# Low halves of the weights made by a second pass of ScalarE and a DMA that adds, in one layer of a hybrid decoder on one core

## The chip, the core and the metric

The kernel runs on one core of a Trainium2 chip. A core has TensorE (PE, with a row of its own, PEld, for weight loads), VectorE (DVE), ScalarE (ACT), GpSimd (POOL), SyncE (SP) and 16 DMA engines that all queues share. Each engine works through its own queue in order. The metric is the time on the device in microseconds (us); less is better. Two runs of the kernel before took 1355.51 and 1356.83 us, median 1356.17.

## What is computed

One layer of a decoder for 512 tokens of 1024 features, everything in float32. Cut to its products:

```
h = h + 0.5 * swiglu(rms_norm(h, ffn1_norm[l]), ffn1_w_gu[l], ffn1_w_down[l])     # 1024 -> 2 x 2816 -> 1024
n = rms_norm(h, mix_norm[l])
p = n @ w_in[l] + b_in[l]                                                         # 1024 -> 6 x 1024
y_a = conformer_conv_branch(...)    # GLU, causal depthwise conv (31 taps), layer norm, swish, @ w_a_out
y_b = spatial_gating_branch(...)    # gelu, layer norm, 128x128 mixing over tokens, @ w_b_out
h = h + (sigmoid(g_a) * y_a + sigmoid(g_b) * y_b) @ w_out[l]
h = h + memory_cross_attention(...) # @ w_q; memory of 256 tokens @ w_kv; 4 heads; @ w_o
h = h + 0.5 * swiglu(rms_norm(h, ffn2_norm[l]), ffn2_w_gu[l], ffn2_w_down[l])
return rms_norm(h, final_norm)
```

## The kernel before

Activations lie transposed: features on the 128 partitions, the 512 tokens along the rows. TensorE works on a float32 form of reduced precision (`F32R`), so each operand is split into a high half (the value rounded to `F32R`) and a low half (the value minus its high half), and a product of two operands takes three matmuls (`mm3`, L103): high times high, high times low of the activations, low of the weights times high. The third of each K tile is the one that needs the weights' low half (L106; L173 in `linear_rows`).

The weights come in blocks of up to 128 x 1024 numbers (512 KB): eight K tiles of 128 columns, or two K tiles of 512 columns. `wload` (L100) does for each block what `wfetch` and `wsplit` do: a DMA on SP's queue into one of four `raw` buffers (L88), ScalarE's copy, rounded, into one of three `whi` buffers (L96), and VectorE's subtraction into one of three `wlo` buffers (L97). Each tile's name follows its product: `g3w0l` is the low half of the first block of the gate product 3. `part`, `linear` and `linear_rows` call `wload`; `linear_pair` and the first two pairs of products call `wsplit` themselves.

In order of time the products are: the gated up-projections g and u of the first half-step FFN (22 each; one block per product), its down-projections d (8; blocks of 1024, 1024 and 768 columns of `raw`), the memory's keys `pk0` to `pk5` (one block each, moving only 256 columns), the input projection (`av`, `ag` by features; `r` by tokens), the two last keys, the gates `gb`, the mixing over tokens, w_b (`yb`), the gates `ga`, the memory's values `pv` (eight blocks of two K tiles, for 256 tokens), w_a (`ya`), w_out (`o`), the queries `pq`, the heads with w_o between them (`wo`; some of its blocks are cut to 768, 512 or 256 columns so that they fit between the heads), and the second FFN. The convolution's 240 vector operations (L344) are spread over the blocks from `av` on by `spend` (L113), which counts a split of a block as 1.14 us of vector work.

A norm's `1/sqrt` is a `pow` of a few columns on GpSimd (L196), in the middle of a chain over PE, VectorE, GpSimd, VectorE, PE and ScalarE (`rstat`, L199). GpSimd's queue has otherwise nine DMAs in all: the mixing weights `wsr` and eight rows broadcast over the partitions (`br`, `gr`, `bb`; 256 KB each).

The order of each engine's queue is not that of the code line by line: a scheduler places the instructions by its own estimate of their lengths, so that it shifts where an operation changes.

Of the kernel before, what the change touches and what calls it, by code (L numbers as in the profile page):

```python
# [11 lines left out]
F32R = mybir.dt.float32r  # L12
AF = mybir.ActivationFunctionType
ALU = mybir.AluOpType
PSUM = bass.MemoryType.PSUM

P = 128
# [13 lines left out]
EPS_RMS = 1e-6  # L31
EPS_LN = 1e-5

# lengths that the order of issue goes by: a K tile's products of 512 columns, a block's split, a vector operation
MM_US, SPLIT_US, OP_US = 0.65, 1.14, 0.66

VECS = [("ffn1_norm", 8), ("mix_norm", 8), ("xattn_norm", 8), ("mem_norm", 8), ("ffn2_norm", 8),
# [10 lines left out]
def conformer_layer(ctx: ExitStack, tc: tile.TileContext, xT, memT, vecs, rows, w_gu1, w_dn1, w_in_f, w_in_t,  # L48
# [31 lines left out]
        return tmp.tile([P, n], dt, tag="ev", name=name, bufs=5)  # L80

    def wfetch(srcs, name):
        """the blocks [128, K tiles, 128 or 512 columns] one after the other in one tile"""
        raw = wpool.tile([P, 1024], F32, tag="raw", name=name, bufs=4)
        n = 0
        for src in srcs:
            m = src.shape[1] * src.shape[2]
            nc.sync.dma_start(out=raw[:, n:n + m], in_=src.rearrange("p k c -> p (k c)"))  # L88
            n += m
        return raw[:, :n]  # L90
# [7 lines left out]
        return hi.rearrange("p (k c) -> p k c", c=c), lo.rearrange("p (k c) -> p k c", c=c)  # L98

    def wload(src, name):  # L100
        return wsplit(wfetch([src], name), src.shape[2], name)

    def mm3(out, whi, wlo, ahi, alo, start, stop):  # L103
        PE.matmul(out, whi, ahi, start=start, stop=False)  # L104
        PE.matmul(out, whi, alo, start=False, stop=False)  # L105
        PE.matmul(out, wlo, ahi, start=False, stop=stop)  # L106

    # steps of vector work that may run at any time (generators that give each step's length) stand behind the
    # blocks of weights, as many as the products of a block leave room for; soon: in order, first; later: by turns
    soon, later = deque(), deque()  # L110
    room = [None]

    def spend(us):  # L113
        """vector work us long has been issued; positive room is filled with steps"""
        if room[0] is not None:
            room[0] = min(room[0], 4.0) - us
            while (soon or later) and room[0] > 0:
                steps = soon or later
                used = next(steps[0], None)
                if used is None:  # L120
                    steps.popleft()
                    continue
                room[0] -= used
                if steps is later and len(steps) > 1:
                    steps[0], steps[1] = steps[1], steps[0]
# [7 lines left out]
        return ps.tile([P, T], F32, tag="mm", name=name)  # L133

    def part(acc, wsrc, ahi, alo, k0, k1, name):
        """K tiles k0 to k1 of a product with wsrc [128, K tiles, 128 columns] stationary, activations moving."""
        nk = wsrc.shape[1]
        whi, wlo = wload(wsrc[:, k0:k1, :], f"{name}w{k0}")
        for k in range(k0, k1):
            mm3(acc, whi[:, k - k0, :], wlo[:, k - k0, :], ahi[k], alo[k], k == 0, k == nk - 1)  # L140
        spend(SPLIT_US - MM_US * (k1 - k0) * acc.shape[1] / T)

    def linear(wsrc, ahi, alo, name, n=T):
        """a whole product: PSUM tile [128 columns, n]"""
        nk = wsrc.shape[1]
        acc = new_ps(name)[:, :n]
        for k0 in range(0, nk, 8):
            part(acc, wsrc, ahi, alo, k0, min(nk, k0 + 8), name)
        return acc

    def linear_pair(wsrcs, ahi, alo, name):
        """two products side by side, K tile by K tile, for activations that come one by one"""
        accs = [new_ps(f"{name}{i}") for i in range(2)]
        for k0 in range(0, DT, DT // 2):
            ks = slice(k0, k0 + DT // 2)
            whi, wlo = wsplit(wfetch([w[:, ks, :] for w in wsrcs], f"{name}w{k0}"), P, f"{name}w{k0}")
            for k in range(k0, k0 + DT // 2):
                for i in range(2):
                    c = i * DT // 2 + k - k0
                    mm3(accs[i], whi[:, c, :], wlo[:, c, :], ahi[k], alo[k], k == 0, k == DT - 1)  # L160
        return accs

    def linear_rows(wsrc, ahi, alo, ntok, name):
        """activations stationary, wsrc [128, K tiles, 512 columns] moving: PSUM tiles [128 tokens, 512]."""
        nk = wsrc.shape[1]
        accs = [new_ps(f"{name}{t}") for t in range(ntok)]
        for k0 in range(0, nk, 2):
            whi, wlo = wload(wsrc[:, k0:k0 + 2, :], f"{name}w{k0}")
            for k in (k0, k0 + 1):
                for t in range(ntok):  # L170
                    a_h, a_l = ahi[k][:, t * P:(t + 1) * P], alo[k][:, t * P:(t + 1) * P]
                    PE.matmul(accs[t], a_h, whi[:, k - k0, :], start=k == 0, stop=False)  # L172
                    PE.matmul(accs[t], a_h, wlo[:, k - k0, :], start=False, stop=False)  # L173
                    PE.matmul(accs[t], a_l, whi[:, k - k0, :], start=False, stop=k == nk - 1)  # L174
            spend(SPLIT_US - MM_US * 2 * ntok)
        return accs
# [20 lines left out]
        return r  # L197

    def rstat(accs, n, eps, name, copy=True):  # L199
        """accs [128, n]: per partition sums of squares. 1/sqrt(mean + eps) as columns [128 tokens, n/128] and as  # L200
        rows on all partitions [128, n]."""
        nt = n // P
        pc = ps2.tile([P, T], F32, tag="st", name=name + "c")[:, :nt]
        for t in range(nt):
            for i, acc in enumerate(accs):
                PE.matmul(pc[:, t:t + 1], acc[:, t * P:(t + 1) * P], avg[:, 0:1], start=i == 0, stop=i == len(accs) - 1)
        ms = tmp.tile([P, TT], F32, tag="ms", name=name + "m", bufs=2)[:, :nt]
        V.tensor_scalar(out=ms, in0=pc, scalar1=eps, scalar2=None, op0=ALU.add)
        rc = pow_mhalf(ms, nt, name + "r")
        dg = ev(name + "d", n)  # L210
        for t in range(nt):
            V.tensor_scalar(out=dg[:, t * P:(t + 1) * P], in0=ident, scalar1=rc[:, t:t + 1], scalar2=None, op0=ALU.mult)
        pb = ps2.tile([P, T], F32, tag="st", name=name + "b")[:, :n]
        PE.matmul(pb, ones, dg, start=True, stop=True)
        if not copy:
            return rc, pb
        rb = tmp.tile([P, n], F32, tag=f"rb{n}", name=name + "rb", bufs=1)
        S.copy(out=rb, in_=pb)  # L218
        return rc, rb
# [2 lines left out]
        split_scaled(xhi[:, m, :], xlo[:, m, :], h[:, m, :], col(g, m))  # L222

    def prep(m, g, acc):
        """residual tile m is final: operands of the next product and its part of the norm."""
        split_x(m, g)
        add_square(acc, h[:, m, :], m == 0)

# [20 lines left out]
        return hi, lo  # L249

    def ffn_up(w_gu, rb, first=()):
        """the hidden activations, split; first: products of the first pairs that are already there"""
        f = [gate_up(pg, pu, rb, j) for j, (pg, pu) in enumerate(first)]
        for j in range(len(first), FT):
            pg = linear(w_gu[j], xh, xl, f"g{j}")
            pu = linear(w_gu[FT + j], xh, xl, f"u{j}")
            f.append(gate_up(pg, pu, rb, j))
        return [a for a, _ in f], [b for _, b in f]
# [1 line left out]
    def add_half(m, pd, ts=slice(0, T)):  # L260
        V.scalar_tensor_tensor(out=h[:, m, ts], in0=pd, scalar=0.5, in1=h[:, m, ts], op0=ALU.mult, op1=ALU.add)  # L261

    # the first two pairs of products go along with the loads, K tile by K tile
    HF = DT // 2
    raws = []
    for k in range(DT):
# [66 lines left out]
    aps, cv, done = [], {}, []  # L333

    def conv(i):
        """causal depthwise convolution of a channel tile; tap k reaches CW - 1 - k tokens back"""
        c = slot(f"cv{i}")
        cv[i] = c
        for back in range(CW):
# [8 lines left out]
            V.tensor_tensor(out=csum, in0=done[0] if len(done) == 2 else csum, in1=c, op=ALU.add)  # L348
        yield OP_US

    # gated channels
    room[0] = 0
    for i in range(DT):
        pv = linear(w_in_f[i], xh, xl, f"av{i}")
# [6 lines left out]
        spend(OP_US)  # L361
        later.append(conv(i))

    # spatial gating unit, tokens on partitions
    wsr = slot("wsr")
    nc.gpsimd.dma_start(out=wsr, in_=sgu_wT.rearrange("s g t -> s (g t)"))
    # [s, t]: kept where t >= s
    wsr3 = wsr.rearrange("s (g t) -> s g t", g=GROUPS)
    G.affine_select(out=wsr3, in_=wsr3, compare_op=ALU.is_ge, fill=0.0, base=0, pattern=[[0, GROUPS], [1, P]],
                    channel_multiplier=-1)  # L370
# [6 lines left out]
        return t  # L377

    def token_major(which):
        """gelu of 1024 columns of the input projection: tiles [token tile][column half]"""  # L380
        out = [[None, None] for _ in range(TT)]
        for half in range(2):
            br = row(which, half, f"br{which}{half}")
# [64 lines left out]
        obl.append(lo)  # L448
        spend(OP_US)

    # the rest of the keys and the values of the memory, and the steps of the spatial gating in between
    vts = [[None, None], [None, None]]

    def value(half):
# [26 lines left out]
            gate_b(TT + k // 2)  # L481
        transposed_u(k)

    # sigmoid(gate_B) * y_B
    for m in range(DT):
        py = linear(w_b[m], obh, obl, f"yb{m}")
        V.tensor_tensor(out=sgb[m], in0=py, in1=sgb[m], op=ALU.mult)
# [8 lines left out]
    finish(later)  # L496
    room[0] = None

    # layer norm over channels, swish
    pmean = ps2.tile([P, T], F32, tag="st", name="pmean")  # L500
    PE.matmul(pmean, avg, csum, start=True, stop=True)
    mean = ev("mean")
# [20 lines left out]
        aah.append(hi)  # L523
        aal.append(lo)

    # sigmoid(gate_A) * y_A, merge
    mgh, mgl = [], []
    py01 = linear_pair([w_a[0], w_a[1]], aah, aal, "ya")
    for m in range(DT):
# [40 lines left out]
        return hi, lo  # L570

    def softmax(hd):
        """probabilities [128 tokens, memory], two token tiles side by side"""
        out = []
        for t2 in range(0, TT, 2):
            sc = ps2.tile([P, 2, NM], F32, tag="st", name="sc")
# [49 lines left out]
            V.tensor_tensor(out=h[:, m, :], in0=po[m], in1=h[:, m, :], op=ALU.add)  # L626
            prep(m, "ffn2_norm", acc)

    # independent products stand between the steps of a head
    q = {}  # L630

    def fill(i):
# [26 lines left out]
    for m in range(last):  # L659
        add_half(m, linear(w_dn2[m], fh, fl, f"d{m}"))  # L660
        add_square(acc, h[:, m, :], m == 0)
        S.activation(h[:, m, :], h[:, m, :], AF.Copy, scale=col("final_norm", m))
    # the last product and the final norm by halves of the tokens
    ws = [wload(w_dn2[last][:, k0:min(FT, k0 + 8), :], f"dl{k0}") for k0 in range(0, FT, 8)]
    for i in range(2):
        ts = slice(i * T // 2, (i + 1) * T // 2)
# [74 lines left out]
```

## Time and profile before

| | |
|---|---|
| time, median of two runs | 1356.17 us |
| span of the profiled execution | 1355.1 us |
| PE busy | 1332.3 us (98%), 5968 matmuls |
| weight loads of PE busy | 1079.1 us (80%) |
| VectorE busy | 777.9 us (57%) |
| ScalarE busy | 456.5 us (34%) |
| GpSimd busy | 19.4 us (1%) |
| mean granted clock of TensorE | 0.996 |
| moved by DMA | 132.47 MB, mean 98 GB/s |

The span goes from the first to the last instruction of the profiled execution. "Busy" counts an engine's own operations; an engine that is 98% busy on the chain that ended last is what sets the time, as long as nothing else makes it wait. A row with `<-` names what a wait ended with.

### The profile page before, as it was taken

To read this page: it belongs to the slowest core of one execution; us is meant where nothing else is said; L and a number is where in the kernel's file an instruction comes from. 1 tells how busy PE (TensorE), PEld (TensorE's weight loads), DVE (VectorE), ACT (ScalarE), POOL (GpSimd) and SP (SyncE) were. 2 spreads that over 40 slices of the span, in tenths; PEclk is the share of its full clock that TensorE was granted. 3 is DMA by queue.
4 is the path that set the end of the run, shared out by engine and by line. 5 is a ranking of instruction groups with operands and counts; after the bars stand their busy time and mean duration, and the time that the engine had idled before them with its cause. 6 is when DMAs were issued, how large, how long until landed. Compare 5 with 4: busy or idle time off the path is not lost.

```text
span 1355.1 us, 14923 instructions
## 1 busy us (share of the span) xinstructions
PE 1332.3 (98%) x5968; PEld 1079.1 (80%) x5968; DVE 777.9 (57%) x1078; ACT 456.5 (34%) x618; POOL 19.4 (1%) x31
## 2 busy tenths in 40 slices
PE   7999999999999999999999999999999999999996
PEld 6788888888898888888787788887878888888886
DVE  5544444434367999998996775554644444442323
ACT  5322222223233223343224743334432222222221
POOL 0000000000020000100000000000000000000000
PEclk9999999999999999999999999999999999999998
DMA  6333333233353332322233333202332333323321
GB/s 207 109 94 93 94 93 94 86 96 109 114 181 115 94 94 94 101 97 76 92 94 116 102 109 109 62 20 76 123 93 93 94 94 93 94 86 101 86 70 62
DMA packets 40660, 132.47 MB, mean 98 GB/s; under 512 B 4432, under 2 KB 7248, under 8 KB 40592
## 3 DMA queue, kind: packets, MB, share of 16 engines
q1 hardware_dynamic: 39872, 129.17, 30.9%
q0 software_dynamic: 720, 2.36, 0.6%
q8 instruction: 46, 0.75, 0.2%
q14 instruction: 22, 0.18, 0.0%
HBM read 129.42 MB, written 2.10 MB: 97 GB/s over the span
## 4 chain that ended last, share of the span: by engine, by line
PE 97%; DVE 1%; ACT 1%; DMA 0%; issue 0%; SPq 0%; DVEq 0%; POOLq 0%; ACTq 0%
PE u L106 6%; PE g L104 6%; PE u L105 6%; PE g L105 6%; PE g L106 6%; PE u L104 6%; PE d L106 6%; PE d L104 6%; PE d L105 6%; PE r L173 2%; PE r L172 2%; PE r L174 2%; PE ya L104 1%; PE ya L105 1%; PE o L105 1%; PE av L105 1%
## 5 line engine op out<-in xcount | busy, mean ns | idle before, releaser
L344 DVE SCALAR_TENSOR_TENSOR cv<-ap,vec,cv 128x494 f32<-128x494 f32 (+24 forms) x240 | 163.3, 729 | 0.4
L244 DVE TENSOR_TENSOR u<-u,n4rb 128x512 f32<-128x512 f32 x22 | 15.2, 692 | 70.3 <-PE u L106 70.3
L244 DVE TENSOR_TENSOR u<-u,n1rb 128x512 f32<-128x512 f32 x20 | 13.8, 691 | 65.8 <-PE u L106 65.8
L240 DVE TENSOR_TENSOR g<-g,n4rb 128x512 f32<-128x512 f32 x22 | 15.2, 692 | 51.7 <-PE g L106 47.5
L240 DVE TENSOR_TENSOR g<-g,n1rb 128x512 f32<-128x512 f32 x20 | 13.8, 691 | 43.3 <-PE g L106 43.3
L246 DVE TENSOR_TENSOR f<-s,u 128x512 f32<-128x512 f32 x44 | 30.4, 692 | 5.4 <-ACT s L242 1.1
L261 DVE SCALAR_TENSOR_TENSOR h<-d,h 128x512 f32<-128x512 f32 x15 | 10.4, 692 | 31.5 <-PE d L106 31.5
L242 ACT ACTIVATE s<-g 128x512 f32<-128x512 f32 x44 | 27.8, 633 | 0.1
L192 DVE TENSOR_TENSOR acc<-acc,sq 128x512 f32<-128x512 f32 x34 | 23.3, 685 | 0.1
L191 ACT ACTIVATE sq<-h 128x512 f32<-128x512 f32 x34 | 21.2, 624 | 1.4 <-DVE h L261 0.2
L184 DVE SCALAR_TENSOR_TENSOR xlo<-h,vec,xhi 128x512 fp32r<-128x512 f32 x24 | 17.7, 746 | 5.3 <-ACT xhi L183 5.2
L183 ACT ACTIVATE xhi<-h,vec 128x512 fp32r<-128x512 f32 x24 | 17.2, 717 | 1.9 <-DVE h L626 1.0
L543 DVE TENSOR_TENSOR h<-o,h 128x512 f32<-128x512 f32 x8 | 5.5, 692 | 13.7 <-PE o L106 13.7
L532 DVE TENSOR_TENSOR ga<-ya,sga 128x512 f32<-128x512 f32 x8 | 5.5, 690 | 13.4 <-PE ya L106 13.4
L387 DVE TENSOR_TENSOR uv<-r,br 128x512 f32<-128x512 f32 x16 | 10.7, 686 | 0.1
L104 PE MATMUL fg<-xhi,first0h 128*128 128x512 f32 x4 | 2.2, 553 | 7.8 <-ACT first0h L96 7.8
L587 ACT ACTIVATE pr<-sc,mx 128x256 f32<-128x256 f32 x16 | 7.4, 470 | 6.4 <-DVE mx L584 6.3
L567 DVE TENSOR_TENSOR qt<-pq,n3rb 128x512 f32<-128x512 f32 x8 | 5.3, 687 | 7.3 <-ACT n3rb L218 4.3
L626 DVE TENSOR_TENSOR h<-wo,h 128x512 f32<-128x512 f32 x8 | 5.4, 688 | 7.0 <-PE wo L106 7.0
L388 ACT ACTIVATE uv<-uv 128x512 f32<-128x512 f32 x16 | 9.0, 621 | 0.6 <-DVE uv L387 0.6
L583 DVE TENSOR_REDUCE mx<-sc 128x2 f32<-128x512 f32 x8 | 5.5, 692 | 3.7 <-PE sc L106 3.3
L97 DVE TENSOR_TENSOR d1w8l<-d1w,d1w8h 128x1024 fp32r<-128x1024 f32 x2 | 2.5, 1226 | 8.7 <-ACT d1w8h L96 8.7
(4300 smaller groups left out, 4279.4 us busy)
## 6 DMA issues: line engine op xcount, KB each, us to landing
h<-xT SPq DMA_DIRECT2D x8, 256.0 KB, 5.9
first<-w_gu SPq DMA_DIRECT2D x8, 256.0 KB, 6.1
d0w<-w_dn SPq DMA_DIRECT2D x4, 512.0 KB, 3.5
d1w<-w_dn SPq DMA_DIRECT2D x4, 512.0 KB, 3.7
d2w<-w_dn SPq DMA_DIRECT2D x4, 512.0 KB, 3.4
d3w<-w_dn SPq DMA_DIRECT2D x4, 512.0 KB, 3.5
d4w<-w_dn SPq DMA_DIRECT2D x4, 512.0 KB, 3.6
d5w<-w_dn SPq DMA_DIRECT2D x4, 512.0 KB, 3.4
```

Source lines behind the costliest of these rows:

```text
L104: PE.matmul(out, whi, ahi, start=start, stop=False)
L105: PE.matmul(out, whi, alo, start=False, stop=False)
L106: PE.matmul(out, wlo, ahi, start=False, stop=stop)
L172: PE.matmul(accs[t], a_h, whi[:, k - k0, :], start=k == 0, stop=False)
L173: PE.matmul(accs[t], a_h, wlo[:, k - k0, :], start=False, stop=False)
L174: PE.matmul(accs[t], a_l, whi[:, k - k0, :], start=False, stop=k == nk - 1)
L192: V.tensor_tensor(out=acc, in0=acc, in1=sq, op=ALU.add)
L240: V.tensor_tensor(out=g1, in0=pg, in1=rb, op=ALU.mult)
L242: S.activation(s1, g1, AF.Silu)
L244: V.tensor_tensor(out=u1, in0=pu, in1=rb, op=ALU.mult)
L246: V.tensor_tensor(out=f, in0=s1, in1=u1, op=ALU.mult)
L344: V.scalar_tensor_tensor(out=o, in0=aps[i][:, :T - back], scalar=w, in1=o, op0=ALU.mult, op1=ALU.add)
```

## The change

`wload` no longer calls `wsplit`. ScalarE makes the high half as before, and then, in a second pass over the same block, the negative high half into the `wlo` buffer. A DMA issued from GpSimd's queue then reads the block of weights from memory once more and adds it to what lies in that buffer, which leaves the weights minus their high half. `linear_pair` and the first products keep `wsplit` with VectorE. Lines from `wload` on are seven further down.

```diff
     def wload(src, name):
-        return wsplit(wfetch([src], name), src.shape[2], name)
+        raw = wfetch([src], name)
+        n, c = raw.shape[1], src.shape[2]
+        hi = wpool.tile([P, 1024], F32R, tag="whi", name=name + "h", bufs=3)[:, :n]
+        lo = wpool.tile([P, 1024], F32R, tag="wlo", name=name + "l", bufs=3)[:, :n]
+        S.copy(out=hi, in_=raw)
+        S.activation(lo, raw, AF.Copy, scale=-1.0)
+        G.dma_start(out=lo, in_=src.rearrange("p k c -> p (k c)"), accum_op=ALU.add)
+        return hi.rearrange("p (k c) -> p k c", c=c), lo.rearrange("p (k c) -> p k c", c=c)
```

The rest of the diff takes comments and docstrings away. The built program has 239 blocks that go this way: 214 of 1024 columns, 19 of 768, one of 512 and five of 256.

GpSimd's queue around the norm of the mixing block (`n2`). Before, the `pow` steps of three norms follow each other:

```order
L196 TENSOR_TENSOR n1r<-n1m,mhalf 128x4
L196 TENSOR_TENSOR nmr<-nmm,mhalf 128x2
L196 TENSOR_TENSOR n2r<-n2m,mhalf 128x4
L366 DMA wsr<-sgu_wT 128x512
L369 AFFINE_SELECT wsr<-wsr 128x512
```

Now, at the keys:

```order
L107 DMA pk0w0l<-w_k 128x1024
L107 DMA pk1w0l<-w_k 128x1024
L107 DMA pk2w0l<-w_k 128x1024
L107 DMA pk3w0l<-w_k 128x1024
L203 TENSOR_TENSOR n2r<-n2m,mhalf 128x4
L107 DMA pk4w0l<-w_k 128x1024
L107 DMA pk5w0l<-w_k 128x1024
L107 DMA av0w0l<-w_in_f 128x1024
```

Each block's DMA stands in the one queue with the norms' steps; each waits there for ScalarE's second pass.

ScalarE's queue where the last short blocks of w_o (256 columns) meet its first full one, `wo4`. Before:

```order
L96 CAST wo2w6h<-wo2w_6956 128x256
L179 CAST oo6h<-po 128x512
L179 CAST oo7h<-po 128x512
L96 CAST wo3w6h<-wo3w_6974 128x256
L96 CAST wo4w0h<-wo4w_6993 128x1024
L96 CAST wo5w0h<-wo5w_7030 128x1024
```

Now:

```order
L186 CAST oo6h<-po 128x512
L186 CAST oo7h<-po 128x512
L105 CAST wo2w6h<-wo2w_7121 128x256
L106 ACTIVATE wo2w6l<-wo2w_7121 128x256
L105 CAST wo3w6h<-wo3w_7140 128x256
L106 ACTIVATE wo3w6l<-wo3w_7140 128x256
L105 CAST wo4w0h<-wo4w_7160 128x1024
L106 ACTIVATE wo4w0l<-wo4w_7160 128x1024
```

Each block has two passes there, and three stand ahead of the one that starts `wo4`'s low half, where before one did.

PE's queue at the same place. Before:

```order
L104 MATMUL wo_6897<-oo7h,wo3w6h 128x512
L105 MATMUL wo_6897<-oo7l,wo3w6h 128x512
L106 MATMUL wo_6897<-oo7h,wo3w6l 128x512
L104 MATMUL wo_6992<-oo0h,wo4w0h 128x512
L105 MATMUL wo_6992<-oo0l,wo4w0h 128x512
L104 MATMUL wo_7029<-oo0h,wo5w0h 128x512
L105 MATMUL wo_7029<-oo0l,wo5w0h 128x512
L106 MATMUL wo_6992<-oo0h,wo4w0l 128x512
```

Now:

```order
L112 MATMUL wo_7159<-oo0l,wo4w0h 128x512
L113 MATMUL wo_7059<-oo6h,wo3w6l 128x512
L111 MATMUL wo_7059<-oo7h,wo3w6h 128x512
L112 MATMUL wo_7059<-oo7l,wo3w6h 128x512
L113 MATMUL wo_7059<-oo7h,wo3w6l 128x512
L111 MATMUL wo_7197<-oo0h,wo5w0h 128x512
L112 MATMUL wo_7197<-oo0l,wo5w0h 128x512
L113 MATMUL wo_7159<-oo0h,wo4w0l 128x512
```

The first matmuls of `wo4`'s high half now stand ahead of those that need `wo3`'s low half. Between the last matmul of `wo1` and the first one with `wo4`'s low half 16 matmuls stand.

## Rows read from the trace of the kernel before

**Rows 1.** The page: busy us, share of the span, instructions of each engine.

```profile
PE 1332.3 (98%) x5968; PEld 1079.1 (80%) x5968; DVE 777.9 (57%) x1078; ACT 456.5 (34%) x618; POOL 19.4 (1%) x31
```

**Rows 2.** The page: the chain that ended last, by engine.

```profile
PE 97%; DVE 1%; ACT 1%; DMA 0%; issue 0%; SPq 0%; DVEq 0%; POOLq 0%; ACTq 0%
```

**Rows 3.** PE's waits: who waited for whom, us in total, times, longest.

```profile
PE fg L104 <- ACT first0h L96: 7.8, 1, 7.8
...
PE ya L104 <- ACT aa0h L179: 1.3, 1, 1.3
...
PE wo L106 <- DVE wo4w0l L97: 0.2, 1, 0.2
```

**Rows 4.** Timeline, second FFN: start us, us, engine, line, operation, out<-in, [idle before].

```profile
1004.06 1.05 ACT L96 CAST g4w0h<-g4w 128x1024 fp32r<-128x1024 f32 x1 [3.95 <-PE u L105]
...
1004.10 0.40 PE L104 MATMUL g<-xhi,g3w0h 128*128 128x512 f32 x1
...
1005.70 1.22 DVE L97 TENSOR_TENSOR g4w0l<-g4w,g4w0h 128x1024 fp32r<-128x1024 f32 x1
...
1009.70 0.40 PE L104 MATMUL u<-xhi,u3w0h 128*128 128x512 f32 x1
```

**Rows 5.** Stretches: length, busy us (instructions) by engine, clock, DMA share, GB/s.

```profile
10.00:12.00 2.00, 2.00 (x6) 1.55 (x5) 1.87 (x3) 1.84 (x3) 0.00 (x0) 1.00 1.06 406
...
740.00:770.00 30.00, 28.72 (x121) 22.10 (x120) 23.83 (x32) 24.14 (x36) 0.00 (x0) 1.00 0.46 142
```

**Rows 6.** The page: SP's DMA queue: packets, MB, share of 16 engines' span.

```profile
q1 hardware_dynamic: 39872, 129.17, 30.9%
```

**Rows 7.** DMA issues: KB each, median us to landing; last, `br` alone.

```profile
u17w<-w_gu SPq DMA_DIRECT2D x2, 512.0 KB, 3.5
...
wsr<-sgu_wT POOLq DMA_DIRECT2D x1, 256.0 KB, 3.9
...
DMA to landing us min/median/max: 3.8/5.2/8.1
```

**Rows 8.** Timeline of GpSimd: two of the broadcast DMAs.

```profile
395.79 1.11 POOL L376 DMA_DIRECT2D br<-rows  x2
```

**Rows 9.** The keys: ScalarE's timeline; PE by tile (ns min/median/max, first to last start).

```profile
381.44 1.05 ACT L96 CAST pk2w0h<-pk2w 128x1024 fp32r<-128x1024 f32 x1 [3.10 <-PE d L105]
...
L104 PE MATMUL pk<-m0h,pk4w0h x2: 277/279/281, 395.4 to 395.7; 128*128 128x256 f32 x2
...
L104 PE MATMUL pk<-m0h,pk5w0h x2: 278/280/281, 398.2 to 398.5; 128*128 128x256 f32 x2
...
L105 PE MATMUL pk<-m6l,pk5w0h x2: 280/280/281, 400.4 to 400.8; 128*128 128x256 f32 x2
```

**Rows 10.** Timeline of PE: first and last matmul of the values.

```profile
731.64 0.40 PE L172 MATMUL pv<-pv0w0h,m0h 128*128 128x512 f32 x1
...
755.53 0.40 PE L174 MATMUL pv<-pv1w6h,m6l 128*128 128x512 f32 x1
```

**Rows 11.** Timeline at w_o's last short block.

```profile
943.56 0.41 ACT L96 CAST wo3w6h<-wo3w 128x256 fp32r<-128x256 f32 x1 [2.74 <-PE wo L105]
```

**Rows 12.** Timeline of PE: last matmul of r01w6, first of gb0.

```profile
580.19 0.39 PE L174 MATMUL r<-r01w6h,xlo 128*128 128x512 f32 x1
...
586.03 0.39 PE L104 MATMUL gb<-xhi,gb0w0h 128*128 128x512 f32 x1
```

## The prediction

> **What bounds the kernel now.** I read the busy times first: PE is busy for 1332.3 of 1355.1 us, DVE for 57% and ACT for 34% [rows 1]. The chain that ended last says the same in another way: 97% of it is PE, 1% DVE, 1% ACT [rows 2]. Then I read PE's waits, to see who ever kept it waiting: 7.8 us at the start (the first weights), 1.3 us before w_a's products (for ScalarE's `aa0`), and for a low half made by VectorE 0.2 us in the whole execution, at `wo4` [rows 3]. So VectorE's subtractions (L97) cost PE next to nothing, and all that PE idles is 1355.1 - 1332.3 = 22.8 us, or 1.7%.
>
> Next I read one ordinary block of weights, since the change is made once per block. A block is 24 matmuls of 512 columns, one each 0.233 us, 5.6 us together: PE begins `g3` at 1004.10 and `u3` at 1009.70 [rows 4]. The moment PE ends a block, its `whi` and `wlo` buffers (three of each) come free for the block three places on: ScalarE makes `g4`'s high half at 1004.06 in 1.05 us, VectorE its low half from 1005.70 in 1.22 us, and PE wants it after two more blocks, at 1015.3. I call the time from a buffer's release to its new low half the **lead needed** (D); what PE takes for the two blocks between is the lead there is, 11.2 us. Before, D is about 2.9 us here. That spare time pays for the change, and where blocks are short it is not there.
>
> **The change part by part.** *Removed:* 239 subtractions on VectorE of at most 1.22 us [rows 4], at most 292 us of its 778. Nothing waits for it but the 0.2 us above, so I give the removal 0. PE's pace in the stage with the convolution, where VectorE is busiest, is the full one as well, so there is nothing to give back there.
>
> *Added on ScalarE:* 239 passes of about 1.05 us (the high half's cast, same shape [rows 4]), at most 251 us on top of 456: 52% of the span. In an ordinary block they are hidden. Only in 740 to 770 is it tight: ACT is busy for 24.1 of 30 us there [rows 5], and some six passes of blocks bring it to 30.4. I charge 1 us.
>
> *Added on GpSimd's queue:* 239 DMAs with an add. The descriptors of a 256 KB DMA took 0.55 us of POOL [rows 8]; 1.1 us per block of 5.6 us is hidden. Some stand ahead of small `pow` steps of the norms (L196, now L203): `n2r` comes behind `pk3`'s DMA and ahead of `pk4`'s, so that `pk4` to `av0` queue behind a step that waits for VectorE, which waits for PE's `n2c`. That is answered about when `pk4` could go anyway: 0.
>
> *Added on the DMA engines:* the weights are read from memory twice, and the low halves are read and written where they lie. A block's plain load takes 524 KB at 406 GB/s = 1.3 us of all engines at their fastest [rows 5] and 0.31 x 5.6 = 1.7 us at their mean [rows 6]. The add has no row here. It can't take less than a plain load (1.3 us), and with two reads and a write each as long as a load at its mean it takes 5.1. I take two passes, 2.6 us: 2.6 + 1.7 = 4.3 of 5.6 us, so the engines don't become the bound.
>
> *How long until it lands* (L, issue to landing) decides. Bound from below: a 512 KB load on SP's queue lands in 3.5 us. From above: one 256 KB DMA of POOL's queue among seven took 8.1 us, and a whole block with an add beside other traffic could take 10. The nearest row is the lone 256 KB load of POOL's queue, 3.9 us [rows 7]; the other half block at 406 GB/s adds 0.65, a second pass 1.3. I take L = 5.9. The Trainium skill (Collectives: The Full Stack, "The bandwidth ceiling: the fold count and why AG ≠ RS ≠ AR") says that an add in the DMA path halves the rate because two sources are read, not because the addition costs time; no run here shows it yet. The Trainium skill (DMA: Bandwidth & Descriptors, "Anatomy of one DMA") gives a DMA of GpSimd about 2.0 us plus its bytes at 436 GB/s, so an estimate by it is 3.2 us for a plain block, where the row has 3.9 us for half of one; by the page the time would come out as in the second rival below.
>
> So D = 2 x 1.05 + 5.9 = 8.0 us. Block for block:
> - Ordinary blocks have 11.2 us of lead, the w_down products (5.6, 5.6 and 4.2 us) 9.8: **0**.
> - `pk0` to `pk5` have 256 columns, 2.8 us each (395.4 to 398.2), and with the norms' small matmuls the six run from 381.5 to 401.0, 19.5 us [rows 9], of which 0.4 (`nmc`) is now earlier. From PE's end of d7: `pk2` can't start before D (its buffer is freed there), ends at D + 2.8, `pk5` takes over its buffer and ends at 2D + 5.6 = 21.6. Loss 21.6 - 19.1 = **2.5 us**.
> - The eight blocks of w_v have 12 matmuls, 2.8 us, and run from 731.6 to 755.8, 24.1 us [rows 10]. The same chain: `pv2` at D, `pv5` at 2D + 2.8, the last of them ends at 2D + 11.2 = 27.2. Loss **3.1 us**. 1.3 us comes back, since `aa0`, for which PE waited after them [rows 3], is then there.
> - `wo4` follows four blocks of 256 columns (1.4 us). From the end of wo3w0: PE does 28 matmuls (6.5 us) before `wo4`'s first low half. Its buffer, wo1w6's, is free after 12 (2.8 us), ScalarE is held by wo3w6's two passes of 0.41 [rows 11] until 3.1, so it lands at 3.1 + 8.0 = 11.1. Loss **4.6 us**; ScalarE's order, shown with the change, has the two passes ahead of it, and PE's has the 16 matmuls behind those 12.
> - `gb0`: buffer free at 580.4, first low half wanted at 586.5 [rows 12]: lead 6.1, loss **1.9 us**.
> - The five broadcast DMAs of 256 KB that stand between r00w2's and r00w4's adds on POOL's queue: **1 us**, a guess from the 8.1 us above.
>
> Sum: 2.5 + 3.1 - 1.3 + 4.6 + 1.9 + 1 + 1 = 12.8 us. The profiled execution's 1355.1 becomes 1368; the median lies 1.1 us above that span, so **1369 us**, +0.9%.
>
> **The rivals.** *The add lands late* (slower). One mechanism: every block's low half comes later than its three buffers allow. As a function of D the short blocks cost 6D - 35; w_down products begin to lose at D = 9.8 (15 of them, D - 9.8 each), the other full blocks of 5.6 us at D = 11.2 ((D - 11.2)/3 each; 166 of them, the 214 blocks of 1024 columns without 32 of w_down, 8 of w_k and 8 of w_v). It is over 2% (27 us) from D = 10, L = 7.9. At L = 10, D = 12.1: 37.6 + 34.5 + 49.8 = 122, **1478 us**. For it: the 8.1 us of a smaller DMA on that queue. Against it: that one stood behind six others, while here they come one per 5.6 us.
>
> *Hidden nearly everywhere:* with L = 4.5 (a plain load's price) D is 6.6; `wo4` still loses 3.2 and `gb0` 0.5, the others nothing: **1360 us**.
>
> *The engines become the bound:* with 5.1 us per add and 1.7 per load, a block of 1024 columns takes 6.8 us of DMA; some 230 such make 1564 us, and the start and end some 40: **about 1600 us**. For it: nothing shows an add's price. Against: the fastest row leaves 4.3 us for it.
>
> *VectorE's relief pays:* over 2% needs more than all of PE's idle 22.8 us, most of it at the start and the end, where no subtraction stands. Nearly excluded.
>
> **How the numbers follow.** 2% is about what a measurement of this kernel can tell from no change. Forecast (L of 5 to 7.9, 1362 to 1383): 0.46; hidden nearly everywhere: 0.12; lands late: 0.29; engines bound: 0.11; faster: 0.02. Slower by over 2% is 0.29 + 0.11 = 0.40, within 2% 0.58, faster 0.02. The range goes from 1357 (L = 3.5, where only `wo4` pays) up to 1490, which takes in the late case at L = 10 and leaves out the engines' case and the worst of the late one, about 0.17, with 0.02 below. The likeliest case's own range is 1362 to 1383.
>
> **What would show it.** The add's issue to landing: 5 to 7.9 us by the forecast. PE's waits: new rows for DMA landings at `pk`, `pv`, `wo` and `gb0`, none in the gated products; `u3` 5.6 us after `g3` still. ACT near 700 us, DVE near 490. Wrong if PE waits in the ordinary blocks (late), if the share of the DMA engines is near full (bound), or if L is under 4.5.

## The result, and the profile after the change

The changed kernel takes **1404.59 us** (two runs, 1401.97 and 1407.2) against 1356.17: a ratio of 1.0352, 95% interval 1.0317 to 1.0388. Five more runs in a later comparison gave 1401.18 us beside 1356.49 (1.0326, 1.0301 to 1.0352). It is slower by 3.3 to 3.5%, where the prediction said 1369 us and "within 2%". The time is inside the stated range of 1357 to 1490, in which 1404.59 lies between the forecast's own 1362 to 1383 and the 1478 of the late rival.

The profiled execution's span is 1400.3 us, 45.2 above the span before. The lines of the page that answer to [rows 1, 2, 6] are these: busy us by engine, the chain by engine, and the two DMA queues with packets, MB and share of 16 engines (q0 is GpSimd's queue, q1 SP's).

```profile
PE 1343.7 (96%) x5968; PEld 1083.2 (77%) x5968; DVE 522.0 (37%) x839; ACT 667.2 (48%) x857; POOL 225.5 (16%) x270
...
q0 software_dynamic: 35136, 122.96, 48.8%
q1 hardware_dynamic: 39872, 129.17, 32.1%
...
PE 70%; issue 17%; DMA 8%; POOL 3%; DVE 1%; ACT 1%; POOLq 0%; SPq 0%; DVEq 0%; ACTq 0%
```

Two things stand in the first line. PE's idle time is 1400.3 - 1343.7 = 56.6 us, 33.8 more than before. And PE's *busy* time, for the same 5968 matmuls, rose by 11.4 us (1332.3 to 1343.7). Together that is the 45.2. The prediction counted waiting only.

Who kept PE waiting (the view of [rows 3]: us in total, times, longest) is now mostly the landing of an add:

```profile
PE po L111 <- ACT ph L186: 3.7, 4, 1.5
PE wo L113 <- DMA wo4w0l<-w_o: 3.6, 1, 3.6
PE pv L180 <- DMA pv0w4l<-w_v: 3.2, 1, 3.2
...
PE pv L180 <- DMA pv1w4l<-w_v: 2.5, 1, 2.5
PE ag L113 <- DMA ag1w0l<-w_in_f: 2.5, 1, 2.5
PE r L180 <- DMA r11w2l<-w_in_t: 2.4, 1, 2.4
PE gb L113 <- DMA gb0w0l<-w_in_f: 2.4, 1, 2.4
PE ya L111 <- ACT aa0h L186: 2.1, 1, 2.1
PE pk L113 <- DMA pk1w0l<-w_k: 1.8, 1, 1.8
PE pk L113 <- DMA pk4w0l<-w_k: 1.8, 1, 1.8
PE wo L113 <- DMA wo3w0l<-w_o: 1.8, 1, 1.8
PE d L113 <- DMA d2w0l<-w_dn: 1.6, 1, 1.6
```

In a block of the gated products nothing is lost. This is the timeline of the block shown in [rows 4], 46.8 us later:

```profile
1050.90 1.05 ACT L105 CAST g4w0h<-g4w 128x1024 fp32r<-128x1024 f32 x1 [3.07 <-PE u L112]
...
1050.93 0.40 PE L111 MATMUL g<-xhi,g3w0h 128*128 128x512 f32 x1
...
1051.86 1.05 ACT L106 ACTIVATE g4w0l<-g4w 128x1024 fp32r<-128x1024 f32 x1
...
1053.20 0.87 POOL L107 DMA_DIRECT2D g4w0l<-w_gu  x1 [4.73 <-ACT g4w0l L106]
...
1056.53 0.40 PE L111 MATMUL u<-xhi,u3w0h 128*128 128x512 f32 x1
```

And these are the DMA issues of two blocks of that kind (KB each, median us from issue to landing); the first is an add, the second the plain load that took 3.5 us in [rows 7]:

```profile
g12w0l<-w_gu POOLq DMA_DIRECT2D x2, 512.0 KB, 7.6
...
u17w<-w_gu SPq DMA_DIRECT2D x2, 512.0 KB, 5.8
```

The buffer is free at 1050.90, the add is issued 2.3 us later and lands 7.5 us after that: D is 9.8 us, against a lead of 11.2. `u3` begins 5.60 us after `g3`, as before. From `g10` to `d1` of either FFN the difference between the two traces does not move by 0.1 us (0.0 in the first, 46.8 in the second).

So the 45 us are lost outside these stretches, nearly all of them between the FFNs. I summed what each start of a matmul stands above the usual spacing (0.233 us, half of it for 256 columns), by place, after minus before: `pk1` to `pk5` 5.7, `ag1` 4.0, `r11` 3.9, `r00` 1.7, `gb0` 2.5, `yb3` 1.2, `pv` 11.3, `ya` 2.2, `po` 1.4, `wo` 9.8, and `d2` of the first FFN 1.8; the final norm's matmuls gave 1.5 back. Of the 9.8 at `wo`, 4.9 stand at `wo4` itself and the rest at three blocks ahead of it (`wo3w0` 2.0, `wo2w6` 1.5, `wo3w6` 1.4). These are figures of one execution. In a second profile of the same kernel (span 1405.1 us) `pk`, `pv` and `wo` lose 6.0, 10.6 and 9.3 us, but `ag` 1.4 (4.0 in the first), `r` 8.5 (5.9) and the w_down products 8.0 (2.1).

Most of the 11.4 us that PE is busy longer has a cause of its own. These are stretches of the changed kernel: length, busy us (instructions) of PE, PEld, DVE, ACT, POOL, granted clock, DMA share, GB/s. The first four are at `wo4`, the others at `ag1`, `r11`, `pv0w4`, `ya` and `gb0`.

```profile
989.00:992.50 3.50, 0.00 (x0) 0.00 (x0) 2.49 (x5) 3.50 (x6) 1.34 (x2) 0.99 1.03 269
992.60:994.00 1.40, 1.40 (x3) 1.12 (x4) 0.89 (x2) 0.03 (x1) 0.05 (x1) 0.50 1.12 260
994.00:995.00 1.00, 1.00 (x4) 0.80 (x3) 0.00 (x0) 0.00 (x0) 0.00 (x0) 0.50 1.02 205
...
996.00:998.00 2.00, 2.00 (x10) 1.63 (x9) 0.00 (x0) 0.00 (x0) 0.00 (x0) 1.00 1.06 268
...
429.80:432.60 2.80, 2.80 (x7) 2.22 (x8) 2.66 (x5) 0.00 (x0) 0.00 (x0) 0.50 1.04 269
...
531.30:535.00 3.70, 3.70 (x10) 2.89 (x11) 3.70 (x7) 0.00 (x0) 0.00 (x0) 0.54 0.54 174
765.80:769.80 4.00, 4.00 (x13) 3.14 (x14) 0.00 (x0) 1.08 (x2) 0.00 (x0) 0.67 1.04 258
791.20:795.50 4.30, 3.98 (x10) 2.79 (x10) 3.17 (x6) 4.30 (x8) 0.00 (x0) 0.62 0.89 173
...
608.40:611.00 2.60, 2.60 (x12) 2.10 (x13) 2.07 (x4) 0.00 (x0) 0.00 (x0) 1.00 1.01 227
```

And this is PE's timeline at `wo4`:

```profile
988.61 0.39 PE L112 MATMUL wo<-oo0l,wo5w0h 128*128 128x512 f32 x1
992.56 0.79 PE L113 MATMUL wo<-oo0h,wo4w0l 128*128 128x512 f32 x1 [3.56 <-DMA wo4w0l<-w_o]
993.15 0.63 PE L111 MATMUL wo<-oo1h,wo4w0h 128*128 128x512 f32 x1
...
996.00 0.39 PE L112 MATMUL wo<-oo3l,wo4w0h 128*128 128x512 f32 x1
```

PE stands still for 3.56 us; when it goes on, the granted clock is 0.50, the 1.2 GHz level, for some three microseconds, and matmuls follow each other at 0.43 us in place of 0.233. At 996.0 the clock is 1.00 again. That costs 1.6 us on top of the wait. The same stands behind the waits at `ag1` (0.50), `r11` (0.54), `pv0w4` (0.67 in a stretch that reaches past it) and `ya` (0.62): five places with some 1.3 to 1.8 us each, about 8 of the 11.4 us; the rest I haven't placed. Behind `gb0`'s wait of 2.35 us the clock stayed at 1.00, behind `r11`'s of 2.37 it fell, so the price can't be read from the wait's length alone. In the second profile the clock fell to 0.50 at `d2`, `r00w4`, `ya` and `wo4`, and not at `ag1`, `r11` or `pv0w4`.

### The profile page after: what moved, and what is told of

It is laid out like the page before. It is cut to its first block, busy times and chain, and to the rows that moved or that the text cites. A ratio compares the mean times of both kernels' runs of the same rounds, so it can differ in the third digit from the quotient of the medians.

```text
span 1400.3 us, 15450 instructions
## 1 busy us (share of the span) xinstructions
PE 1343.7 (96%) x5968; PEld 1083.2 (77%) x5968; DVE 522.0 (37%) x839; ACT 667.2 (48%) x857; POOL 225.5 (16%) x270
## 3 DMA queue, kind: packets, MB, share of 16 engines
q0 software_dynamic: 35136, 122.96, 48.8%
q1 hardware_dynamic: 39872, 129.17, 32.1%
## 4 chain that ended last, share of the span: by engine, by line
PE 70%; issue 17%; DMA 8%; POOL 3%; DVE 1%; ACT 1%; POOLq 0%; SPq 0%; DVEq 0%; ACTq 0%
PE g L111 4%; PE u L111 4%; PE u L112 4%; PE g L113 4%; PE g L112 4%; PE u L113 4%; PE d L113 4%; PE d L112 4%; PE d L111 4%; PE o L111 1%; PE o L113 1%; PE o L112 1%; PE gb L113 1%; PE ga L111 1%; PE ga L112 1%
## 5 line engine op out<-in xcount | busy, mean ns | idle before, releaser
L351 DVE SCALAR_TENSOR_TENSOR cv<-ap,vec,cv 128x493 f32<-128x493 f32 (+23 forms) x240 | 165.0, 733 | 5.6 <-ACT cv L349 3.1
L190 ACT ACTIVATE xhi<-h,vec 128x512 fp32r<-128x512 f32 x24 | 17.0, 710 | 0.8 <-DMA h<-xT 0.8
L441 DVE SCALAR_TENSOR_TENSOR uv<-pm,vec,uv 128x256 f32<-128x256 f32 x16 | 7.0, 480 | 23.8 <-PE pm L113 23.8
L366 DVE SCALAR_TENSOR_TENSOR ap<-av,vec,ag 128x512 f32<-128x512 f32 x8 | 6.0, 751 | 19.0 <-ACT ag L364 19.0
```

The costliest lines, as they stand in the source:

```text
L190: S.activation(hi, src, AF.Copy, scale=g)
L351: V.scalar_tensor_tensor(out=o, in0=aps[i][:, :T - back], scalar=w, in1=o, op0=ALU.mult, op1=ALU.add)
```

## Experiments

My theory (A): the loss is the add's landing, L, put into D = 2.1 us + L, wherever the three buffers give less lead than D. Against it stood (B) the load of the DMA engines, (C) ScalarE's second pass, (D) GpSimd's queue with the row broadcasts in it. All times are medians, beside 1356.2 to 1356.5 us of the kernel before on the same chip; the letters are those of the expectations.

**The same DMA without the add.** The low half is then the weight itself, the subtraction is left out.

```
-        G.dma_start(out=lo, in_=src.rearrange("p k c -> p (k c)"), accum_op=ALU.add)
+        G.dma_start(out=lo, in_=src.rearrange("p k c -> p (k c)"))
```

> Every low half is loaded by the same DMA on GpSimd's queue, but without the add, over ScalarE's negative pass (the low half is then the whole weight: the subtraction is left out). Queue, order, bytes from HBM, ScalarE's passes and all waits stay. Theory A (all of the loss is the add's landing, 7.6 us after its issue in the median, so a lead needed D of 2.1 + 7.6 = 9.7 us where short blocks give less): a plain load should land after 3.9 + 0.65 = about 4.5 us, D = 6.6, and the loss goes from 48 to about 8: 1360 to 1368 us; PE's waits for pk and pv gone, wo4 and gb0 left with about 3 and 1 us. Rival C (ScalarE's second pass and what queues behind it): nothing changes, 1400 to 1406. Rival D (GpSimd's queue, its order and the broadcasts in it): nothing changes, 1398 to 1406. Rival B (two reads of the weights from HBM load the DMA engines): the landing falls little, 1390 or more.

Measured: 1368.18 us, ratio 1.0095 (1.0078 to 1.0111), at the upper edge of what theory A gave. Same queue, same order, same bytes, and 33 to 36 of the 45 to 48 us are gone: C and D can't carry the main part. GpSimd's queue on this kernel's page, and the DMA issues in the places of two adds:

```profile
q0 software_dynamic: 35136, 122.96, 25.7%
```

```profile
g12w0l<-w_gu POOLq DMA_DIRECT2D x2, 512.0 KB, 4.5
...
r11w2l<-w_in_t POOLq DMA_DIRECT2D x1, 512.0 KB, 4.2
```

A plain block lands after 4.5 us, the figure that the prediction had worked out for a plain load (3.9 + 0.65). The add lands after 7.6. What the add adds is 3.1 us of landing, not the 1.3 that I had put down for "a second pass". On the engines it takes 0.488 x 1400.3 / 122.96 MB x 0.524 = 2.9 us per block, plain 0.257 x 1368.7 / 122.96 x 0.524 = 1.5: a factor of 1.94.

**The add in the FFNs alone, and everywhere else alone.**

```
     def wload(src, name):
+        if not (name[0] in "gud" and (name[1].isdigit() or name[1] == "l")):   # the second kernel: without "not"
+            return wsplit(wfetch([src], name), src.shape[2], name)
```

> The add is kept for the 132 or so blocks of the two FFNs (g, u, d) alone; all other low halves come from VectorE as before the change. Theory A: those blocks have 9.8 to 11.2 us of lead against D = 9.7, only d2 loses (1.9 us): 1357 to 1360 us. Rival B (the DMA engines' load of the adds) or C (ScalarE's passes): each add costs its share, 132 of 239, 1375 to 1385 us.

> The other way round: the FFNs' blocks go back to VectorE, the 107 others (memory's keys and values, convolution branch, gating branch, merge, attention) keep ScalarE's negative pass and the add. Theory A: nearly the whole loss stands there, 1400 to 1405 us. Rivals B and C (a price per add): 107 of 239, 1375 to 1382 us.

Measured: 1357.37 us (1.0016, 1.0006 to 1.0026) and 1400.0 us (1.0325, 1.0311 to 1.0339). The adds in the FFNs, with the DMA engines at 8 to 9 tenths there, cost 1 us; the others cost the whole loss. There is no fixed price per add. The only low half that PE waited for in the first of the two for more than 0.3 us is `d2`'s:

```profile
PE d L115 <- DMA d2w0l<-w_dn: 2.3, 1, 2.3
```

**ScalarE's negative pass with VectorE's addition behind it, no DMA.**

```
-        G.dma_start(out=lo, in_=src.rearrange("p k c -> p (k c)"), accum_op=ALU.add)
+        V.tensor_tensor(out=lo, in0=lo.bitcast(F32), in1=raw, op=ALU.add)
```

> ScalarE's negative pass stays, but VectorE adds the weights to it in SBUF in place of the DMA (no second read, nothing on GpSimd's queue). Theory A: the lead needed is 1.05 + 1.05 + 1.2 = 3.3 us in place of 9.7, below every lead there is: 1355 to 1360 us; d2, where ScalarE's other passes hold the second pass up, may keep 1 us. Rival C (ScalarE's second pass costs the time): 1385 to 1405 us. Rivals B and D: 1356.

Measured: 1365.39 us, 1.0069 (1.0057 to 1.0082). I missed that one: ScalarE's second pass costs 9 us in this kernel, where PE waits for no block's low half; of these I had expected at most 4 and the prediction had charged 1. PE's waits of this kernel that grew show where, all but a few tenths of a us of them for ScalarE:

```profile
PE ya L111 <- ACT aa0h L186: 2.8, 1, 2.8
...
PE av L111 <- ACT av1w0h L105: 1.8, 1, 1.8
...
PE yb L111 <- ACT yb5w0h L105: 1.2, 1, 1.2
```

These are places where ScalarE has other work in front: the normalized activations' halves (`av1`), the convolution's passes and casts before w_a (`ya`). `po`'s four waits for ScalarE's `ph` grew too, from 2.3 to 3.8 us in all. No run shows that VectorE's relief brought anything back: DVE was busy for 782.0 us in this kernel and 522.0 after the change, and the kernel with the add in the FFNs alone, with 132 subtractions fewer than before the change, was no faster either.

**The source of the add in SBUF instead of HBM; the add in two halves.** Two ways to a shorter landing.

```
-        G.dma_start(out=lo, in_=src.rearrange("p k c -> p (k c)"), accum_op=ALU.add)
+        G.dma_start(out=lo, in_=raw, accum_op=ALU.add)                              # the first kernel
+        flat = src.rearrange("p k c -> p (k c)")                                    # the second kernel
+        for i in (0, n // 2):
+            G.dma_start(out=lo[:, i:i + n // 2], in_=flat[:, i:i + n // 2], accum_op=ALU.add)
```

> The add stays, but its source is the copy of the weights that the plain load has already brought into SBUF (`raw`), so nothing is read from HBM a second time. Measured so far: issue to landing of a 512 KB DMA on GpSimd's queue, 4.5 us plain, 7.6 us with the add. Theory A1 (the 3.1 us of difference is the add itself, which handles two sources): landing stays near 7.6 us, 1395 to 1408 us. Rival A2 (it is the second read from HBM beside the plain loads): landing falls to about 5 us, 1368 to 1375 us. `raw` is held longer, by the add's landing, so a slower result than after the change would come from the loads being issued later.

> Each add is issued as two DMAs of half the columns (256 KB), the half that PE wants first ahead; ScalarE's passes stay whole. Theory A (the landing decides, and grows with the bytes): the first half lands about 5.5 us after its issue in place of 7.6, the second half comes about 2 us later, while PE is on the first; D falls by about 2 us, and at some 24 us per 4 us of D (6D - 35) 10 to 14 us come back: 1388 to 1396 us. Rival D (GpSimd's queue and its descriptors, twice as many instructions): 1404 or slower, up to 1420. If a DMA's fixed part or the queue's other entries decide, the first half lands no earlier than 7 us and the time stays at 1400 to 1408.

Measured: 1384.92 us (1.0218, 1.0195 to 1.024) and 1392.39 us (1.0269, 1.0253 to 1.0284). The halves are inside theory A's range. With the source in SBUF the landing lies between the two theories (issue to landing of `g12`'s add by its tile; then the queue's line of the page):

```profile
DMA to landing us min/median/max: 5.2/5.6/6.1
```

```profile
q0 software_dynamic: 35136, 122.96, 48.9%
```

`g12`'s landing fell from 7.6 to 5.6 us, the median of the adds of `g10` to `u19` from 7.6 to 6.1 (4.5 without the add), the time by 16 to 20 us. Neither A1 nor A2 is right alone: about half of the add's extra landing goes with the second read from HBM, the rest stays with the add. The plain loads of `g10` to `u19` landed earlier as well (5.1 us in the median, 7.4 after the change), so part of what the second read costs may be the load that it puts on the engines. But the engines' time did not fall (48.9%), so the doubled engine time is the add's, wherever the source lies. By halves, the landing of `g12`'s adds is 5.0 to 6.0 us, and GpSimd issues for 440.7 us in place of 225.5, while the time falls all the same.

**Both at once.** The halves are added from `raw`.

> Both changes that made the landing shorter at once: the add reads the copy of the weights in SBUF (alone: landing about 6.0 us in place of 7.6, 1384.9 us) and is issued in two halves (alone: first half after about 5.8 us, 1392.4 us). Theory A (time follows the landing of what PE wants first, some 11 to 12 us of time per us of landing): the first half lands after about 4.5 us and the time is 1368 to 1376 us. Rival D (GpSimd's queue, with 0.87 us per DMA, is what is left): no better than SBUF alone, 1383 to 1390 us.

Measured: 1379.34 us, 1.017 (1.0156 to 1.0184). Between the two expectations: 5.6 us better than SBUF alone, not the 9 to 17 of theory A. The landings fell (`g12`: 3.3 to 6.1, median 4.4), but `pv0w4` still waits 3.9 us, as with SBUF alone. So time does not simply follow the first half's landing.

**A fourth buffer for high and low halves,** and its control: the kernel before the change with the same pools. To make room, both have three buffers in place of four for the loaded weights (`raw`) and 48 in place of 50 for activations; the lines below are those of the halves.

```
-        hi = wpool.tile([P, 1024], F32R, tag="whi", name=name + "h", bufs=3)[:, :n]
-        lo = wpool.tile([P, 1024], F32R, tag="wlo", name=name + "l", bufs=3)[:, :n]
+        hi = wpool.tile([P, 1024], F32R, tag="whi", name=name + "h", bufs=4)[:, :n]
+        lo = wpool.tile([P, 1024], F32R, tag="wlo", name=name + "l", bufs=4)[:, :n]
```

> The changed kernel with four buffers for the high halves and four for the low ones in place of three; to make room, three in place of four for the loaded weights and 48 in place of 50 for activations. Theory A (lead needed against lead there is): each block's add is issued one block earlier, the lead grows by 2.8 us for short blocks and 5.6 us for full ones; 6D - 35 at 9.7 us loses most of its 23 us, so do ag1, r11 and d2; what is left is ScalarE's part (about 9 us, measured) and bursts at pv: 1362 to 1375 us. Rival B (the DMA engines or GpSimd's queue are short of throughput in these stages): more buffers do not help, 1395 to 1405 us.

> The kernel before the change (VectorE makes all low halves) with the buffers of the run with four: the control for it. Theory A: VectorE's low halves were in time with three, so a fourth and fewer others change nothing: 1355 to 1359 us. If the smaller pools cost time by themselves it is above that, and the run with four is to be read against this one.

Measured: 1378.43 us (1.0162, 1.0147 to 1.0178) and 1358.82 us (1.0022, 1.0013 to 1.0032). With the landing unchanged (7.4 to 8.2 us for `g10` to `u19`) the extra lead brings 23 to 26 us back, with the same bytes moved in less time: B, a shortage of throughput, can't be the main part. The time is 3 us outside my range, and 20 us above its control. B isn't gone everywhere. At `pk` and `pv` a block takes PE 2.8 us, and its add and one plain load take the engines 4.7 (an estimate from the queues' shares, 2.9 + 0.321 x 1400.3 / 129.17 x 0.524). In the changed kernel the engines' share is 0.99 from 382 to 407 us (`pk`) and 0.96 from 751 to 787 (`pv`), and the adds of `pv` land after up to 11.3 us. With four buffers `pk` lost 1.0 us in place of 5.9, but `pv` still 4.0, at a share of 0.97 and with landings up to 10.9. How much of `pv`'s loss is the load of the engines no run here separates. The largest wait left for an add is `wo4`'s, as before; its tile (first and last start, then the landing) says why:

```profile
L107 POOL DMA_DIRECT2D wo4w0l<-w_o x1: 863/863/863, 958.1 to 958.1; - x1
...
  PE wo L113: 4.0, 1
...
DMA to landing us min/median/max: 7.3/7.3/7.3
```

Four buffers back from `wo4` are four blocks of 256 columns of weights (six matmuls, 1.4 us each): the lead is a block more, but it is a block of 1.4 us. ScalarE could begin its high half only at 955.80, and the low half landed at 965.4: D = 9.6.

**The row broadcasts on SP's queue,** twice, the second time beside the changed kernel itself.

```
-        nc.gpsimd.dma_start(out=t, in_=rows[i:i + 1, half * T:(half + 1) * T].partition_broadcast(P))
+        nc.sync.dma_start(out=t, in_=rows[i:i + 1, half * T:(half + 1) * T].partition_broadcast(P))
```

> The changed kernel, but the eight row broadcasts of 256 KB (`br`, `gr`, `bb`) are issued on SP's queue in place of GpSimd's. After the change they stand between adds: r11w2's add landed after 10.0 us, r00w4's after 12.4 us, in place of some 7.7, and PE lost 3.9 us at r11 and 1.7 us at r00. Theory A (a neighbour on the same queue makes the add land late): both adds land after about 8 us and 4 to 6 us come back: 1398 to 1401 us. Rival B (the broadcasts take the same DMA engines, whichever queue they come from): the landings and the time stay, 1403 to 1407 us; or the plain loads behind them on SP's queue come late, up to 1410.

> The changed kernel itself once more, to have it on the same chip and in as many runs as the run with the row broadcasts on SP's queue: 1402 to 1407 us by either theory.

> The run with the row broadcasts on SP's queue once more, beside the changed kernel. Theory A (the neighbours on GpSimd's queue made r11's and r00's adds late): 4 to 6 us below the changed kernel of the same call. Rival B (same DMA engines, either queue): no difference beyond 2 us.

Measured: 1398.63 us (1.0319, 1.0294 to 1.0343), then 1397.72 (1.0298, 1.0278 to 1.0317) beside 1401.18 for the changed kernel (1.0326, 1.0301 to 1.0352), which is just under the 1402 that I expected at least. The second 3.5 us lie between the theories, and the intervals overlap, so by the time alone it isn't settled. At the place it is clearer. The landings of r11w2's and r00w4's adds in the changed kernel are, in this order,

```profile
r11w2l<-w_in_t POOLq DMA_DIRECT2D x1, 512.0 KB, 10.0
...
r00w4l<-w_in_t POOLq DMA_DIRECT2D x1, 512.0 KB, 12.4
```

(9.8 and 13.6 us in its second profile), and with the broadcasts on SP's queue 7.0 and 10.0 (8.3 and 10.2). At r11 and r00 PE lost 5.6 and 7.7 us in the two profiles of the changed kernel, and 0 and 0.8 in the two with SP's queue. Over all blocks of `r`, with the waits that then show up at `r10` and `r01`, it lost 5.9 and 8.5 us against 1.1 and 3.8. r00w4's add still lands after 10.0 us and more beside the broadcasts, so part of it is the common engines (B); most of what PE pays for is the neighbour on the same queue, some 4.7 us by these profiles, though the times of the two kernels lie only 2.6 and 3.5 us below 1401.18.

## Why the prediction was wrong

**What held.** PE bounds; the blocks of the gated products lose nothing; nothing shows VectorE's relief to be worth anything; most of the loss stands at `pk`, `pv`, `wo`, `gb0` and the broadcasts; in the blocks of 5.6 us the DMA engines do not become the bound (2.9 + 1.8 = 4.7 us per block, 4.3 predicted); GpSimd's issue (0.87 us, 1.1 guessed) is free. The Trainium skill (Collectives: The Full Stack, "The bandwidth ceiling: the fold count and why AG ≠ RS ≠ AR") has an add halve the rate by its two source reads. The engines' time, 2.9 us against 1.5, agrees, and it stayed at 2.9 with the source in SBUF. The Trainium skill (DMA: Bandwidth & Descriptors, "Anatomy of one DMA") gave an estimate of 3.2 us for a plain block; it took 4.5.

**The step that failed first: L.** The prediction took 3.9 + 0.65 + 1.3 = 5.9 us. The first two terms are right to the tenth (4.5); the add's is 3.1 in place of 1.3, so L is 7.6 and D 9.7. I had set the add's delay equal to its extra time on the engines at their fastest rate. Still, 7.6 lies inside the 5 to 7.9 us that the forecast allowed for L, so this step alone would have left the time inside 1362 to 1383.

**What failed second, and by more: the terms of the sum.** With D = 9.7 the prediction's own formulas give a span of 1378, a time of 1379, still "within 2%"; the other 22 us were not in it.

| place | prediction | its formula at D = 9.7 | measured |
|---|---|---|---|
| `pk` | 2.5 | 5.9 | 5.7 |
| `pv` | 3.1 | 6.5 | 11.3 |
| `wo` | 4.6 | 6.3 | 9.8 |
| `gb0` | 1.9 | 3.6 | 2.5 |
| `aa0`'s wait at `ya` | -1.3 | -1.3 | +2.2 |
| broadcasts (`r11`, `r00`) | 1 | 1 | 5.6 |
| ScalarE's second pass | 1 | 1 | see below |
| `ag1`, `d2`, `yb3`, `po` | 0 | 0 | 8.4 |
| final norm | 0 | 0 | -1.5 |
| sum | 12.8 | 23.0 | 44.0 of 45.2 |

Of the 1.2 us left over, 0.8 stand at w_a's next blocks (`ya2`, `ya3`).

At `pk` the chain of buffers comes out as reasoned. At the others, this was left out:

- *The clock.* Every wait was priced at its length. Behind five of them PE ran at the 1.2 GHz level for about three microseconds, some 8 us in all (`pv`, `wo`, `ya`, `ag1`, `r11`).
- *D isn't one number.* At `pv0w4` it is 11.1 us, since ScalarE puts the gate's `sga` between its two passes and the add lands after 8.2 (the two adds behind it, `pv0w6` and `pv1w0`, after 11.3 and 10.1):

```profile
754.55 1.05 ACT L105 CAST pv0w4h<-pv0w 128x1024 fp32r<-128x1024 f32 x1 [2.31 <-PE ga L112]
755.50 0.68 ACT L500 ACTIVATE sga<-ga,vec 128x512 f32<-128x512 f32 x1
756.09 1.05 ACT L106 ACTIVATE pv0w4l<-pv0w 128x1024 fp32r<-128x1024 f32 x1
...
757.43 0.87 POOL L107 DMA_DIRECT2D pv0w4l<-w_v  x1 [4.73 <-ACT pv0w4l L106]
```

- *The blocks ahead of `wo4`.* The sum had `wo4` alone. `wo3w0`, `wo2w6` and `wo3w6`, whose adds landed 7.5, 4.1 and 4.6 us after their issue, cost 5.0 us more.
- *Full blocks were given 11.2 us of lead by their size alone.* `av0`, `ag0` and `av1` are worked on by turns, while the normalized activations come one by one, so the buffer for `ag1` comes free late, and PE has work for 7.8 of the 10.3 us until the add lands:

```profile
419.41 1.05 ACT L105 CAST ag1w0h<-ag1w 128x1024 fp32r<-128x1024 f32 x1 [7.01 <-issue]
...
421.72 0.86 POOL L107 DMA_DIRECT2D ag1w0l<-w_in_f  x1 [9.19 <-ACT ag1w0l L106]
...
429.76 0.79 PE L113 MATMUL ag<-xhi,ag1w0l 128*128 128x512 f32 x1 [2.49 <-DMA ag1w0l<-w_in_f]
```

- *A pass of ScalarE can be late itself.* `d2`'s two passes stood behind the memory's operands (L190, L195), so that its add was issued only at 284.96.
- *ScalarE.* The second pass costs 9 us without any DMA; the prediction looked at one stretch (740 to 770) and at its sum, not at who stands behind each pass. The 9 us can't simply be added to the rest: in the kernel without the add PE has no wait for `av1w0h`.

**The rivals.** "Lands late" had the right sign and nearly the right landing (over 2% from L = 7.9), but by another place: it let the w_down blocks and the full blocks pay. At D = 9.7 the w_down blocks' 9.8 us held but for `d2`; the short and interleaved blocks paid more than 6D - 35. With the landing of `g10` to `u19` at 4.5, 6.1 and 7.6 us in the median (whole blocks: plain, add from SBUF, add from HBM) the time was 1368, 1385 and 1401 to 1405 us, 10 to 13 us per us of landing, where the formula had 6. The first of these is above the 1360 us of "hidden nearly everywhere", mostly for `pv` and ScalarE. "Engines become the bound" fell for the kernel as a whole with the measured 4.7 us of 5.6; at the blocks of 2.8 us they may be part of the loss.

No variant beat the kernel before. The add in the FFNs alone comes nearest, and it gains nothing: the trace before shows no wait there for VectorE's low halves.

## What to carry to other kernels

Before an engine's pass is replaced by a DMA, write down for each kind of block the time from the buffer's release to its reuse, and compare it with the DMA's landing, and its engines' time with the length of the block; here the blocks of the gated products passed both tests, the short blocks failed both, and the interleaved ones failed the first. Price a wait of PE with what its clock does after it, and take an unmeasured landing from a bound, not from the engines' fastest rate. A busy engine that nobody waits for has nothing to give.

## What the runs showed of the hardware that I had not expected

- A 512 KB DMA of GpSimd's queue landed after 4.5 us plain, 7.6 us with an add from HBM and 6.1 us with an add from SBUF (medians of `g10` to `u19`), while the engines' time for it was 1.5, 2.9 and 2.9 us.
- The plain loads beside the adds got slower too: `u17w` 3.5 to 5.8 us, all of `g10` to `u19` 3.5 to 7.4 in the median, without a cost in those blocks.
- A broadcast DMA of 256 KB beside adds took 8.6 us in the median (`br`; 5.2 before), and the add behind five of them 12.4.
- After 3.56 us without a matmul PE came back at half its clock for about three microseconds; after 2.35 us at `gb0` it did not.
